# V's first weights in tiles of their own, denser fillers and a gated latent projection in a hybrid attention layer

## The chip, the cores and the metric

The kernel runs on one core of one Trainium2 chip. The metric is device time in microseconds (us): the median of several runs. The engines are TensorE (PE: matmuls; PEld: its weight loads), VectorE (DVE), ScalarE (ACT), GpSimd (POOL) and SyncE (SP), which issues the DMAs here. Each engine works through its own instruction list in order. SBUF is the on-chip memory, PSUM the accumulators that PE writes.

## The reference

One encoder layer, 1024 tokens of width 1024, all in float32. Cut to what matters:

```python
mod = silu(c) @ w_ada + b_ada;  sh_a, sc_a, g_a, sh_m, sc_m, g_m = split(mod, 6)
h = modulate(rmsnorm(x, g_attn_norm), sh_a, sc_a)
q_lat, kv_lat, k_rope, ca_qkv = split(h @ w_in)          # 256, 128, 32, 3*8*64 columns
# latent attention: 8 heads, q = norm(q_lat) @ w_q_up, k, v from norm(kv_lat) @ w_kv_up,
# rotary part of 32, QK-norm, block-causal softmax over all earlier 64-token chunks
o_mla = mla_attention(q, k, v)
# chunked attention: 8 heads of 64, QK-norm, a band of 9 chunks, relative-position bias
o_ca = chunk_attention(cq, ck, cv, rel_bias)
x = x + g_a * (concat([o_mla, o_ca]) @ w_out)
h = modulate(rmsnorm(x, g_mlp_norm), sh_m, sc_m)
u = causal_dwconv(h @ w_up, conv_w) + conv_b;  gate, val = split(u)
x = x + g_m * ((silu(gate) * val) @ w_down)
```

## The kernel before

Every float32 product is made of three matmuls. Each operand is split into a high part (rounded to the type PE takes, made by `hi_of`, L74) and the rest (`lo_of`, L82), and high x high, high x low and low x high are added up in PSUM (`gemm3`, L149). So each weight that comes from memory needs a DMA, a high part on ACT, DVE or POOL, and a low part on POOL or DVE, before PE can use it. `load_w` (L174) does that for eight slices of a weight matrix: three raw buffers (tag `wr`) take the DMAs, sixteen buffers (tag `ws`) the split slices.

The program has these stages, in order.

*Start.* The token rows are loaded and normalized, the conditioning vector's product with the first part of `w_ada` is accumulated on DVE (`ada_pair`, L249, weights by `load_ada`), and the modulated, transposed activations `hT` come out slice by slice: for each `d` from 0 to 7 PE transposes, ACT and DVE make the high parts, DVE and POOL the low parts, and PE adds slice `d` to the first query and key projection (`qk0`). Behind that loop `wv0` is loaded and split (L285): V's weights for the first two pairs of heads, with the sums of their squares (`ssw0`), from which a power-of-two scale for V is worked out (`pow2_scale`).

*Attention, with fillers.* Two lists are interleaved. One is the list of attention units. There are 16 chunked units `ca_unit(p, g, o)`: pair of heads `p` (0 to 3), half of the queries `g`, head `o` of the pair. They come in pairs (`o` = 0, 1), eight pairs in all; the seventh is `p` = 3, `g` = 0, the last `p` = 3, `g` = 1. Behind them come 16 latent units `mla_unit(gr, hh, g)`. Each unit has four tiles of 128 queries. A tile's `scores` (L717) are matmuls, a minimum on DVE, an exponential on ACT, a scaling and a split into two half-precision parts on POOL and DVE, and a transposing DMA; its `values` come some tiles later. At a unit's first tile `prep` makes its pages: queries and keys transposed by PE and split again (`ca_pages`, L690).

The other list is the fillers (L899): the V projection of the first heads (`v0`, `f_v`), query and key projections (`qk1`, `qk2`, `qk3`, `f_qk`), `v1`, the low-rank projection (`m`, `f_m`: 192 matmuls of 416 columns, then transposes of the normalized latents into `latT`), the up projections of the two groups of latent heads (`up0`, `up1`, `f_up`) and the chunked heads' part of the output projection (`oca`). Each filler is a generator that yields the cost in ns of what it has just emitted. `pace` (L936) draws from it after each tile: the tile's cost times a ratio, `R_CA` in chunked tiles and `R_MLA` in latent ones. `need` empties the list up to what a unit needs: the first latent unit needs `up0`. Two further generators ride on the fillers: `side` (`f_ada`, the rest of the conditioning, DVE steps named `aacc`) for every 1700 ns of filler, and the rotary tables (`rope_tables`, L483) with `qk1`. The latter works in 14 scratch slots on DVE, with two Sine activations on ACT.

What decides the order on an engine in the end is a scheduler at build time. It takes the order of emission as the priority; scores, softmax and values are lifted above it (`high_priority`). So a page is behind the fillers that were emitted ahead of it.

The tag `pg` has six buffers, which hold in turn rows of `x`, normalized queries and keys (`qns`), the rotary scratch and `latT` (three for each half of the tokens). The transposes of the second half in `f_m` therefore need buffers that the last chunked pages have read.

*Rest.* Output projection, gated multilayer perceptron in a seven-product (Strassen-like) form, down projection. The change doesn't touch these.

Of the kernel before, what the change touches and what calls it, by code (L numbers as in the profile page):

```python
# [12 lines left out]
F32 = mybir.dt.float32  # L13
# [10 lines left out]
P = 128  # L24
# [20 lines left out]
PSCALE, VSCALE = 2.0 ** 15, 2.0 ** 14  # L45
R_CA, R_MLA = 1.9, 0.5

# [16 lines left out]
def layer_kernel(ctx, tc, I, out):  # L64
# [108 lines left out]

    def load_w(name, src, ncol, he="a", ssw=None, jt=None):  # L174
        tiles = []
        for k in range(ND):
# [7 lines left out]
            for c0 in range(0, ncol, 256):  # L184
# [3 lines left out]
                anchor["sp"] = sp.dma_start(rw, src[:, k, c]).ins  # L188
                if jt:
                    junk = jt(f"{name}j{k}")[:, :c.stop - c0]  # L190
                    dve.tensor_tensor_reduce(junk, rw, rw, 1.0, 0.0, MUL, ADD, accum_out=ssw[:, k:k + 1])
                elif ssw is not None:
                    junk = qtile(f"{name}j{k}")
                    act.activation(junk[:, :c.stop - c0], rw, AF.Square, accum_out=ssw[:, k:k + 1])
# [9 lines left out]
    def load_ada(dd, c):  # L204
        w = st.tile([P, 2, 512], F32, name=f"adaw_{dd}_{c}", tag="wa", bufs=5)
        sp.dma_start(w[:], I["w_ada_a"][dd][:, 2 * c:2 * c + 2])
        wada[dd, c] = w
# [39 lines left out]
    ssw0 = cst.tile([P, ND], F32, name="ssw0")  # L247

    def ada_pair(dd):  # L249
        acc = rtile(f"adacc_{dd}")  # L250
# [9 lines left out]
    for d in range(ND):  # L260
        dd, half = divmod(d, 2)
        if half == 0 and dd + 1 < ND // 2:
            for c in range(4):
                load_ada(dd + 1, c)
            ada_pair(dd + 1)
        pt = ps.tile([P, 512], F32, name=f"p_ada{d}", tag="mm", bufs=2)
# [8 lines left out]
        for h in range(2):  # L275
            hT[d, h] = mod_transpose(lambda j: xs[4 * h + j][:, d * P:(d + 1) * P], d, h, 0, ps, ("T", "pv")[h], 1,
                                     hw, "hT", st, 16, "v" if h else "a", "v" if h else "p")
        for t in range(NT):
            h, j = divmod(t, 4)
# [4 lines left out]

    with tc.issue_after(anchor["lov"]), tc.issue_after(anchor["lop"]):  # L285
        wv0 = load_w("wv0_", I["w_v"][0], 256, he="v", ssw=ssw0,
                     jt=lambda n: st.tile([P, 512], F32, name=n, tag="hv", bufs=2))
    startp.__exit__(None, None, None)
# [143 lines left out]

    latT = {}

    def rope_apply(o, x, tab, t, nh, tmp, eng=pool):
# [10 lines left out]
    def f_m():  # L446
# [4 lines left out]
        for t in range(NT):  # L451
# [17 lines left out]
            lat[t] = raw  # L469
            if j == 3:  # L470
                for b in range(3):
                    ptt = ps.tile([P, 512], F32, name=f"lt_ps{h}_{b}", tag="T", bufs=TB)
# [10 lines left out]
    def rope_tables():  # L483
# [4 lines left out]
        def T():  # L488
            n = cnt[0] % 14
            cnt[0] += 1  # L490
            return buf[n // 8][:, n % 8]
# [50 lines left out]
        pi_s = 3.1415925  # L542
        sn, cn, cl, c2, cl2 = T(), T(), T(), T(), T()
        dve.tensor_scalar(cl, tot, pi_s, -pi_s, op0=MIN, op1=MAX)
        dve.tensor_scalar(c2, tot, math.pi / 2, None, op0=ADD)
        yield
        dve.tensor_scalar(cl2, (yield from reduce(c2)), pi_s, -pi_s, op0=MIN, op1=MAX)
        act.activation(sn, cl, AF.Sin)
        act.activation(cn, cl2, AF.Sin)
        yield  # L550
# [311 lines left out]
    def ca_unit(p, g, o):  # L862
        def prep():
# [8 lines left out]
            if o == 0:  # L872
                pages["c", p, g] = ca_pages(p, g)
        u = Unit(f"c{p}{o}", 64 * o, 64,
                 lambda: (pages["c", p, g][0], [pages["c", p, i][1] for i in range(g + 1)]),
# [29 lines left out]
    def fill_step():  # L905
        while fillers:
# [12 lines left out]
            if key not in ("v0", "up0", "up1", "oca"):  # L919
                nside[0] += c  # L920
                while nside[0] > 1700:
# [571 lines left out]
```

## Time and profile before

| | us |
|---|---|
| median of 3 runs | 1419.71 (1411.23 to 1421.71) |
| the profiled execution | 1410.1 |
| its span, first to last instruction | 1408.3 |
| PE busy in the span | 1234.5 |
| DVE busy | 1093.0 |
| POOL busy | 709.3 |
| ACT busy | 624.0 |

The profile is of one execution. Busy time of an engine is the union of its instructions' times. A row of the timeline gives start, duration, engine, line, operation, the tile written and those read, with the idle time before it and what ended that in brackets. A row of busy times by stretch gives, after its bounds and length, the busy time of PE, PEld, DVE, ACT and POOL with the number of instructions, then the TensorE clock that was granted (1 is full), the share of the DMA engines and GB/s. In the names `sc` are scores of chunked units, `sm` of latent ones, `ipv` and `ipq` the projections, `mp` the low-rank one, `qu` and `ku` the up projections; the numbers of buffers are left out.

The stages by the trace: the start up to 68 us, V's first projection up to 101 us, chunked units up to about 392 us, the first up projection up to 424 us, latent units up to 634 us, the output projection up to about 731 us, then the perceptron.

### The profile page before, as it was taken

What the parts mean: (1) busy time and instruction counts of PE and PEld (TensorE: products, weight loads), DVE (VectorE), ACT (ScalarE), POOL (GpSimd) and SP (SyncE); (2) the same over time, 40 slices, a digit from 0 to 9 for tenths busy, and PEclk for the clock granted to TensorE, in tenths of its full rate; (3) what the DMA queues carried; (4) which work ended last, traced back from release to release, by engine and by line L of the source; (5) the groups of instructions that cost most, each with busy time, mean ns of one, the idle gap of its engine ahead of it and who ended that gap; (6) DMA issues with size and microseconds to landing.
All of it is one profiled execution on the core that took longest, in us unless ns stands there. A gap on an engine that the chain in (4) does not pass through costs nothing.

```text
span 1408.3 us, 18699 instructions
## 1 busy us (share of the span) xinstructions
PE 1234.5 (88%) x6156; PEld 1006.3 (71%) x6156; DVE 1093.0 (78%) x1861; ACT 624.0 (44%) x1132; POOL 709.3 (50%) x685
## 2 busy tenths in 40 slices
PE   4879688989777789995677999999999999999998
PEld 3868476978655567774565887787778777888886
DVE  6847879686579997882577888988888888698667
ACT  4433545444456554652274444344434444443331
POOL 5353366375545674443563677677667874200000
PEclk9989798998888889997887999999999999999999
DMA  8223567755221478877721323333232223894451
GB/s 314 93 64 79 132 149 177 169 134 106 57 53 42 88 169 178 164 160 230 279 90 45 113 95 123 127 119 127 91 108 89 101 99 118 303 350 130 125 163 60
DMA packets 223689, 190.56 MB, mean 135 GB/s; under 512 B 148709, under 2 KB 166885, under 8 KB 223593
## 3 DMA queue, kind: packets, MB, share of 16 engines
q1 hardware_dynamic: 223592, 189.38, 47.3%
q8 instruction: 48, 0.79, 0.2%
q14 instruction: 49, 0.39, 0.1%
HBM read 117.24 MB, written 37.49 MB: 110 GB/s over the span
## 4 chain that ended last, share of the span: by engine, by line
DVE 35%; PE 30%; issue 10%; DMA 9%; POOL 8%; ACT 7%; SPq 1%; POOLq 0%; DVEq 0%; ACTq 0%
DVE u L1157 5%; DVE u L1156 4%; PE dnA_P L1304 2%; PE dnA_P L1305 2%; PE dnA_P L1306 2%; ACT u L1155 2%; DVE hlc L794 2%; PE dnB_P L1306 1%; PE dnB_P L1305 1%; PE dnB_P L1304 1%; DVE hlm L794 1%; DMA wor<-w_out 1%; DMA aw<-w_ada 1%; PE sc L740 1%; PE sm L746 1%
## 5 line engine op out<-in xcount | busy, mean ns | idle before, releaser
L76 ACT ACTIVATE dnP<-dnr 128x1024 fp32r<-128x1024 f32 x73 | 77.3, 1062 | 111.8 <-PE dnA_P L1306 43.1
L1278 DVE TENSOR_TENSOR dnP<-dnr,dnP 128x1024 fp32r<-128x1024 f32 x72 | 90.3, 1259 | 44.9 <-ACT dnP L76 43.3
L1156 DVE SCALAR_TENSOR_TENSOR u<-c,cvp,u 128x1023 f32<-128x1023 f32 x44 | 81.9, 1902 | 46.3 <-ACT u L1155 46.3
L72 POOL TENSOR_SCALAR hlm<-Pm,rim 128x512 f16<-128x512 f32 (+2 forms) x96 | 69.8, 736 | 71.8 <-DVE rim L775 28.7
L1157 DVE SCALAR_TENSOR_TENSOR u<-c,cvp,u 128x1022 f32<-128x1022 f32 x44 | 86.5, 2003 | 0.0
L72 POOL TENSOR_SCALAR hlc<-Pc,ric 128x640 f16<-128x640 f32 (+2 forms) x64 | 47.1, 738 | 71.1 <-DVE ric L775 35.4
L794 DVE SCALAR_TENSOR_TENSOR hlm<-Pm,rim,hlm 128x512 f16<-128x512 f32 (+2 forms) x96 | 65.0, 688 | 6.2 <-POOL hlm L72 5.9
L772 ACT ACTIVATE Pc<-sc,mc 128x640 f32<-128x640 f32 (+2 forms) x64 | 42.1, 658 | 54.5 <-DVE mc L761 38.9
L772 ACT ACTIVATE Pm<-sm,mm 128x128 f32<-128x128 f32 (+3 forms) x64 | 47.1, 737 | 32.0 <-DVE mm L765 18.6
L794 DVE SCALAR_TENSOR_TENSOR hlc<-Pc,ric,hlc 128x640 f16<-128x640 f32 (+2 forms) x64 | 53.0, 830 | 10.0 <-POOL hlc L72 9.3
L76 ACT ACTIVATE wc<-ws 128x512 fp32r<-128x512 f32 x22 | 13.9, 633 | 103.1 <-DVE ws L1082 103.1
L1155 ACT ACTIVATE u<-c,cvp 128x1024 f32<-128x1024 f32 x44 | 52.1, 1234 | 13.5 <-DVE c L1228 6.8
L153 PE MATMUL ipq<-wq_s,hT 128*128 128x256 f32 x192 | 56.2, 296 | 1.2 <-ACT wq_s L76 1.2
L154 PE MATMUL ipq<-wq_s,hT 128*128 128x256 f32 x192 | 56.0, 292 | 0.6 <-POOL wq_s L83 0.6
L155 PE MATMUL ipq<-wq_s,hT 128*128 128x256 f32 x192 | 56.1, 292 | 0.0
L833 PE MATMUL pvm<-PTm,vt 128*128 128x256 f16 (+1 forms) x320 | 43.2, 284 | 12.6 <-DMA PTm<-hlm 8.8
L1232 ACT ACTIVATE u<-u 128x1024 f32<-128x1024 f32 x22 | 23.3, 1061 | 67.9 <-DVE u L1157 67.9
L83 POOL TENSOR_TENSOR wc<-ws,wc 128x512 fp32r<-128x512 f32 x22 | 34.3, 1558 | 36.4 <-ACT wc L76 36.4
L1306 PE MATMUL dnA_P<-dnP 128*128 128x512 f32 x132 | 51.4, 389 | 0.0
L1305 PE MATMUL dnA_P<-dnP 128*128 128x512 f32 x132 | 51.4, 389 | 0.0
L1304 PE MATMUL dnA_P<-dnP 128*128 128x512 f32 x132 | 51.2, 389 | 0.0
L83 POOL TENSOR_TENSOR wd<-wu,wd 128x512 fp32r<-128x512 f32 x22 | 30.4, 1382 | 37.5 <-ACT wd L76 37.5
(421 smaller groups left out, 4544.6 us busy)
## 6 DMA issues: line engine op xcount, KB each, us to landing
wu<-w_up SPq DMA_DIRECT2D x44, 512.0 KB, 3.5
dnr<-g_d SPq DMA_DIRECT2D x73, 256.0 KB, 4.3
aw<-w_ada SPq DMA_DIRECT2D x48, 256.0 KB, 3.5
g_d<-u SPq DMA_DIRECT2D x22, 512.0 KB, 2.8
dnr<-w_down SPq DMA_DIRECT2D x44, 256.0 KB, 5.4
adaw<-w_ada_a SPq DMA_DIRECT2D x16, 512.0 KB, 4.9
x<-x SPq DMA_DIRECT2D x16, 512.0 KB, 8.5
g_d<-gs SPq DMA_DIRECT2D x22, 256.0 KB, 2.0
```

What stands on the lines that cost most here:

```text
L72: pool.tensor_scalar(o, i, s, 1.0, op0=MUL, op1=MUL)
L76: act.activation(o, i, AF.Copy)
L83: (pool if eng == "p" else dve).tensor_tensor(o, i, f32(hi), op=SUB)
L772: act.activation(pr[:, :n], sv, AF.Exp, bias=m[:], scale=-1.0, accum_out=rsum[:, 0:1])
L794: dve.scalar_tensor_tensor(hl[:, w:2 * w], pp, ri[:], hl[:, :w], op0=MUL, op1=SUB)
L1155: act.activation(u[:], c, AF.Identity, scale=cvp[:, cv + 2:cv + 3], bias=cvp[:, cv + 3:cv + 4])
L1156: dve.scalar_tensor_tensor(u[:, 1:], c[:, :S - 1], cvp[:, cv + 1:cv + 2], u[:, 1:], op0=MUL, op1=ADD)
L1157: dve.scalar_tensor_tensor(u[:, 2:], c[:, :S - 2], cvp[:, cv:cv + 1], u[:, 2:], op0=MUL, op1=ADD)
L1278: r = f(*a, **k)
L1304: pe.matmul(pt, sh, w[:, 0, 0], start=start, stop=False, skip_group_check=add)
L1305: pe.matmul(pt, sh, w[:, 1, 0], start=False, stop=False, skip_group_check=add)
L1306: pe.matmul(pt, sl, w[:, 0, 0], start=False, stop=stop, skip_group_check=add)
```

## The change

It has five parts. V's first weights get eight raw tiles (`wvr`, in the start's own pool), whose loads stand right behind the last conditioning weights on SP's queue; their splits (high part and sum of squares on DVE, low part on POOL) are emitted two for each `d` from 4 to 7, inside the start's loop. `R_CA` goes from 1.9 to 2.3. In `f_m`, the second half's transposes wait until the pages of the last pair of chunked units have been emitted: the generator yields -1 meanwhile, and `pace` then gives up its debt. So `up0`, which stands behind, is emitted within the last two chunked units and not ahead of the first latent unit. The rotary tables use ten scratch slots, and the arguments of the two Sines lie side by side, so that one activation does both. The argument `jt` of `load_w` goes.

```diff
-R_CA, R_MLA = 1.9, 0.5
+R_CA, R_MLA = 2.3, 0.5
...
-        sp.dma_start(w[:], I["w_ada_a"][dd][:, 2 * c:2 * c + 2])
+        anchor["ada"] = sp.dma_start(w[:], I["w_ada_a"][dd][:, 2 * c:2 * c + 2]).ins
...
+    wv0, wv0r = [], []
+
+    def wv0_load():
+        with tc.issue_after(anchor["ada"]):
+            for k in range(ND):
+                r = st.tile([P, 256], F32, name=f"wv0_r{k}", tag="wvr", bufs=8)
+                anchor["sp"] = sp.dma_start(r[:], I["w_v"][0][:, k, :]).ins
+                wv0r.append(r)
+
+    def wv0_split(k):
+        w = hw.tile([P, 2, 256], F32R, name=f"wv0_s{k}", tag="ws", bufs=16)
+        junk = st.tile([P, 512], F32, name=f"wv0_j{k}", tag="wvj", bufs=1)
+        with tc.issue_after(anchor["lov"]), tc.issue_after(anchor["lop"]):
+            hi_of("v", w[:, 0], wv0r[k][:])
+            lo_of("p", w[:, 1], wv0r[k][:], w[:, 0])
+            dve.tensor_tensor_reduce(junk[:, :256], wv0r[k][:], wv0r[k][:], 1.0, 0.0, MUL, ADD,
+                                     accum_out=ssw0[:, k:k + 1])
+        wv0.append((w[:, 0], w[:, 1]))
...
             for c in range(4):
                 load_ada(dd + 1, c)
+            if dd + 2 == ND // 2:
+                wv0_load()
             ada_pair(dd + 1)
...
+        if d >= ND // 2:
+            for k in range(2 * d - ND, 2 * d - ND + 2):
+                wv0_split(k)
...
-    with tc.issue_after(anchor["lov"]), tc.issue_after(anchor["lop"]):
-        wv0 = load_w("wv0_", I["w_v"][0], 256, he="v", ssw=ssw0,
-                     jt=lambda n: st.tile([P, 512], F32, name=n, tag="hv", bufs=2))
...
+    gate = [False]
...
             if j == 3:
+                while h and not gate[0]:
+                    yield -1
                 for b in range(3):
...
-            n = cnt[0] % 14
+            n = cnt[0] % 10
...
-        sn, cn, cl, c2, cl2 = T(), T(), T(), T(), T()
+        cl, cl2, sn, cn, c2 = buf[1][:, 2], buf[1][:, 3], buf[1][:, 4], buf[1][:, 5], T()
...
-        act.activation(sn, cl, AF.Sin)
-        act.activation(cn, cl2, AF.Sin)
+        act.activation(buf[1][:, 4:6], buf[1][:, 2:4], AF.Sin)
...
                 pages["c", p, g] = ca_pages(p, g)
+                gate[0] = (p, g) == (3, 1)
...
-                nside[0] += c
+                nside[0] += max(c, 0)
...
-            if c is None:
+            if c is None or c < 0:
```

More of the change, by code (lines that the diff above doesn't have):

```diff
@@ L171, in gemm3_f, with load_w @@
             yield 3 * len(part) * max(107, w / 2.4 + 2.5)
-    def load_w(name, src, ncol, he="a", ssw=None, jt=None):
+    def load_w(name, src, ncol, he="a", ssw=None):
         tiles = []
@@ L188, in load_w @@
                 anchor["sp"] = sp.dma_start(rw, src[:, k, c]).ins
[L189 to L192, printed above, removed]
+                if ssw is not None:
                     junk = qtile(f"{name}j{k}")
```

## Prediction

> **What bounds the kernel now.** I read the page first, then the busy time by stretch, cut where the work changes hands, then the instructions at the edges.
>
> ```profile
> span 1408.3 us, 18699 instructions
> PE 1234.5 (88%) x6156; PEld 1006.3 (71%) x6156; DVE 1093.0 (78%) x1861; ACT 624.0 (44%) x1132; POOL 709.3 (50%) x685
> ```
>
> ```profile
> core 0: us, PE busy (x) PEld busy (x) DVE busy (x) ACT busy (x) POOL busy (x), PEclk, DMA share, GB/s
> 68.00:101.00 33.00, 23.10 (x144) 20.67 (x142) 15.93 (x48) 9.78 (x21) 21.11 (x27) 0.79 0.24 73
> ...
> 283.00:320.00 37.00, 33.41 (x215) 28.62 (x213) 30.06 (x72) 15.97 (x36) 27.87 (x29) 0.94 0.56 128
> 320.00:345.00 25.00, 25.00 (x112) 20.66 (x111) 16.88 (x52) 10.14 (x44) 16.77 (x44) 0.82 0.54 120
> 345.00:365.00 20.00, 14.43 (x88) 12.21 (x87) 8.28 (x17) 8.12 (x19) 5.15 (x13) 0.95 0.29 42
> 365.00:388.00 23.00, 21.00 (x98) 16.69 (x97) 14.46 (x45) 11.98 (x37) 16.80 (x35) 0.82 0.38 80
> 388.00:432.00 44.00, 29.96 (x129) 21.57 (x128) 36.28 (x119) 23.96 (x59) 22.02 (x24) 0.84 0.25 55
> 432.00:502.00 70.00, 52.02 (x259) 40.18 (x260) 66.80 (x198) 41.34 (x96) 43.99 (x46) 0.83 0.40 85
> ```
>
> The share on the page (PE 88%) is a mean over unlike stages. From 68 to 101 us (V's first projection) no engine is busy for even three quarters of the time. From 283 to 345 us PE is nearly full. From 345 to 432 us neither PE nor DVE is (44.4 and 44.6 of 64 us up to 345-365 and 388-432, 21.0 and 14.5 of 23 between): work runs one kind after the other there. From 432 to 502 us DVE is the bound, 66.8 of 70. All edits lie before 502 us; behind that I take the kernel as it is, shifted. The edges are these rows of PE (first V product; first page of the chunked attention; its first scores; first scores of the seventh pair of chunked units; scores of the last two units when they get under way; first finished scores of the latent attention):
>
> ```profile
> 68.00 0.28 PE L153 MATMUL ipv<-wv_s,hT 128*128 128x256 f32 x1
> 68.12 0.35 PE L154 MATMUL ipv<-wv_s,hT 128*128 128x256 f32 x1
> ...
> 93.24 0.60 PE L674 MATMUL q_ps<-ident,qn 128*128 128x128 f32 x4
> ...
> 101.20 0.30 PE L740 MATMUL sc<-k,qh 128*128 128x128 f32 x1 [1.64 <-DVE k L705]
> ...
> 319.37 0.31 PE L740 MATMUL sc<-k,qh 128*128 128x128 f32 x1
> ...
> 363.71 0.47 PE L740 MATMUL sc<-k,qh 128*128 128x128 f32 x1 [1.55 <-DVE k L705]
> ...
> 424.85 0.33 PE L746 MATMUL sm<-mk,mq_0h 96*128 96x128 f32 x1 [0.46 <-DVE mk L687]
> ```
>
> **Part 1, V's first weights (-10 us).** These are the eight loads and the splits:
>
> ```profile
> L188 SPq DMA_DIRECT2D wv_r<-w_v x8: 328/328/383, 37.8 to 77.0; - x8
> L191 DVE CUSTOM_DVE_ANT_0 wv_j<-wv_r x8: 405/420/956, 66.6 to 79.8; 128x256 f32<-128x256 f32 x8
> L80 DVE CAST wv_s<-wv_r x8: 279/285/853, 66.9 to 80.1; 128x256 fp32r<-128x256 f32 x8
> L83 POOL TENSOR_TENSOR wv_s<-wv_r,wv_s x8: 724/768/1171, 67.3 to 82.1; 128x256 fp32r<-128x256 f32 x8
> ```
>
> With three raw buffers, the last load is issued at 77.0 us and the last low half starts at 82.1, so the first two V products (96 matmuls) run from 68.0 to 93.2 us. With eight buffers the loads follow the last conditioning weights on SP's queue and nothing holds them. The 96 matmuls at the pitch of the two rows above (68.00 to 68.12, 0.12 us) take 11.5 us; add 1 us for the scale's small matmul and its DVE readers, which stand between the two products. The page then starts at 80.7 instead of 93.24, a gain of 12.5. The moved loads go ahead of the first bias pair and the next projection's weights on SP's queue: eight issues of 0.328 us, 2.6 us. DVE reads the bias, in the built order, ahead of its last conditioning step; what it waits there is within the slip that follows.
>
> The splits now fall into the start, where PE sets the pace:
>
> ```profile
> 56.00:68.00 12.00, 12.00 (x103) 11.99 (x103) 7.45 (x21) 6.30 (x10) 3.43 (x5) 1.00 0.01 2
> ```
>
> DVE has 4.5 us free there and gets 8 x (0.42 + 0.285) = 5.6 us by the medians; POOL has 8.6 free and gets 8 x 0.77 = 6.2. So DVE overruns by 1 us, and by the longest rows (0.956 + 0.853 each, 14.5 us) by 10, of which some 5 could be taken before 56 us or behind the last product. Slip 0 to 6, I take 2.5: -12.5 + 2.5 = -10, ends -12.5 and -6. The longest rows fell where POOL was splitting at the same time. [...]
>
> **Part 2, one Sine instead of two (-2 us).**
>
> ```profile
> 150.81 1.28 ACT L548 ACT_TABLE_LOAD   x1
> 154.40 1.28 ACT L772 ACT_TABLE_LOAD   x1 [1.99 <-DVE mc L761]
> 166.42 1.28 ACT L549 ACT_TABLE_LOAD   x1
> 168.04 1.28 ACT L772 ACT_TABLE_LOAD   x1
> ```
>
> Each Sine costs a load to it and one back. One pair goes, 2.56 us of ACT, with the softmax of the chunked units queued behind it in ACT's order. Ends 0 and -2.9 (Sine's own 0.3 us with it); I take -2, as ACT waits near by anyway. [...] Ten scratch slots instead of 14 cost nothing: all users but the Sine are on DVE, in order.
>
> **Part 3, denser fillers (+22 us before 319, -24 us behind).** In the built program the low-rank projection has 44 of its 192 matmuls ahead of the seventh pair's first scores before the change, and 174 after; the other fillers there are the same. Earlier in the chunked units the orders hardly differ, as the weights, not the ratio, hold the fillers. The matmul's pitch:
>
> ```profile
> 377.58 0.35 PE L153 MATMUL mp<-wm_h,hT 128*128 128x416 f32 x1
> 377.77 0.35 PE L154 MATMUL mp<-wm_l,hT 128*128 128x416 f32 x1
> ```
>
> 130 x 0.19 = 24.7 us. PE idles 3.6 of 37 us in 283:320, so I take 3 as absorbed: +22. Ends +17 (twice the idle time found) and +30 (5 us of waiting for weights). Then the seventh pair and the start of the last one stand almost without fillers: before, 319.37 to 363.71 took 44.3 us. What is left is eight small tiles and the last pages. DVE has 16.88 + 8.28 us of work there, less the conditioning steps, which are now done earlier (seven in the row below, 5.2): 20, and the steps of the latent transposes in it wait at the gate now. The pace of chunked tiles with no filler stands in the second row: seven softmaxes in 24.7 us, of wider tiles, with table loads and pages among them.
>
> ```profile
> L404 DVE SCALAR_TENSOR_TENSOR aacc<-aw,cs,aacc 128x512 f32<-128x512 f32 x7 | 5.2, 746 | 0.4 <-DMA aw<-w_ada 0.4
> ...
> L772 ACT ACTIVATE Pc<-sc,mc x7: 359/793/794, 148.4 to 173.1; 128x640 f32<-128x640 f32 x5, 128x128 f32<-128x128 f32 x1, 128x256 f32<-128x256 f32 x1
> ```
>
> Between 17 and 25 I take 20, DVE's work: -24, ends -27 and -19.
>
> **Part 4, up projection beside the last two units (-13 us), its rest later (+3 us).** Before, 363.71 to 424.85 us is 61.1 us: eight tiles, then eight steps of the up projection alone. The built program now has 27 of the 72 matmuls of that projection among the last tiles and 63 of 72 ahead of the latent scores. DVE's work up to 424.85 is 14.46 + 36.28 less some 6.8 in the last 7.2 us, 44; one step of eight leaves (under 36.28 / 8 = 4.5; I take 3), so 41, and with the latent transposes' steps that now fall here 42 to 44. At the share of 432:502 (95%) 43 us takes 45; at that of 388:432 (82%) 52. I take 48: -13, ends -17 and -8. What is hidden is PE's work: 21.00 x 0.82 + 29.96 x 0.84 = 42 us at full clock, less 42 low-rank matmuls at 0.19 (8 us) that have gone, 34; it decides only if the granted clock falls under 0.7. The step that is left lands where DVE is 95% busy: +3 (0 to +5). The gate itself costs nothing on an engine: it holds back emission, and behind the closed gate stand only the latent transposes and the up projection.
>
> **Sum.** -10 - 2 + 22 - 24 - 13 + 3 = -24. The profiled run took 1410.1 us (span 1408.3 and 1.8 around it), so 1386.1; it lies 0.7% under the median of 1419.71, and scaled to that the forecast is 1395.5.
>
> **Rivals.** *The last two units and the up projection do not overlap.* Every up step waits for POOL in DVE's order, and a chunked tile behind it waits too:
>
> ```profile
> 406.47 1.65 POOL ur L117
> ```
>
> Eight such waits of 1.65 us are 13.2, the whole of part 4. Then -24 + 13 = -11, 1408.6. For it: DVE is in order, and the rows put POOL on the chain. Against: from 432 on the second up projection runs beside attention with the same waits, and DVE is 95% busy.
>
> *The early V is given back.* If the fillers of the chunked units are paced by a transfer that doesn't move with V, part 1 is lost: -14, 1405.6. For it: the second key projection is starved by its weights (first row below; 100 matmuls in 28 us). Against: those weights wait for a Square of the projection ahead, which shifts as well.
>
> *Slower: the filler block starves with attention locked behind it.* Between the first scores of the sixth pair and its key page PE now has 192 projection matmuls and 38 of the low-rank one, in its own order; tiles behind can't pass.
>
> ```profile
> 172.00:200.00 28.00, 16.64 (x100) 14.49 (x101) 0.82 (x2) 0.82 0.72 169
> 267.00:300.00 33.00, 24.55 (x189) 23.12 (x189) 1.79 (x3) 1.00 0.43 99
> ...
> L83 POOL TENSOR_TENSOR wm_l<-wm_r,wm_h x16: 520/737/1402, 266.2 to 317.8; 128x256 fp32r<-128x256 f32 x8, 128x160 fp32r<-128x160 f32 x8
> ```
>
> The block is 192 x 0.12 + 38 x 0.19 = 30 us. At the starved pace of the first row (28 us where 12 would do, 2.3 times) it takes 69: +39, so +15, 1435. It decides from 24 us of stall on. For it: the low-rank weights were split over 51 us. Against: the 189 matmuls of the second row ran at full clock, and their weights are split ahead of the block in POOL's new order too; only the last four low-rank weights wait for buffers that the block frees.
>
> That the change does nothing is excluded by the built order, where up steps do stand among the last chunked tiles.
>
> **Chances.** Forecast 0.72, no overlap 0.12, early V given back 0.10, starved block 0.06. The parts' ends added are -43 and +2; not all fall together, half way gives -34 to -11, so 1385.5 to 1408.6; the runs before spread over 10.5 us, and the two middle rivals lie within. I set 1379 to 1411. Within 1% is what a measurement of this kernel can't tell from none: 1405.5 to 1434. Faster: 0.70 of the forecast, half of the V rival, little of the first: 0.77. Same: 0.17. Slower: 0.06.
>
> **What would show it.** First chunked scores near 91 us instead of 101.2; two Sine loads less; the seventh pair's scores some 10 us later than 319 and then eight tiles in about 20 us with little on PE; latent scores near 398 instead of 425; 432:502 as full on DVE as before. The prediction is wrong if the start's last product ends beyond 72 us, if PE waits for low-rank weights inside the block, or if the last two units with seven up steps take over 56 us.

## The result, and the profile after

Taken side by side in 19 runs each, the changed kernel took 1409.99 us (median, 1405.15 to 1413.90) and the kernel before 1414.45 us (1408.14 to 1427.44): a ratio of 0.9967, 95% interval 0.9951 to 0.9982. The gain is real, but it is 4.5 us where 24 were forecast. The profiled execution took 1407.2 us, 2.9 us less than the profiled one before. The page:

```profile
span 1405.4 us, 18702 instructions
PE 1231.5 (88%) x6156; PEld 1005.2 (72%) x6156; DVE 1093.2 (78%) x1861; ACT 620.9 (44%) x1129; POOL 700.1 (50%) x685
```

Work is as before on DVE, and a little less on PE (3.0 us), ACT (3.1) and POOL (9.2); what the change did, it did by order, but for the one Sine. Busy times by stretch of the changed kernel (columns as in the prediction), cut at its own edges:

```profile
core 0: us, PE busy (x) PEld busy (x) DVE busy (x) ACT busy (x) POOL busy (x), PEclk, DMA share, GB/s
252.00:296.00 44.00, 41.77 (x320) 40.10 (x320) 22.75 (x40) 15.72 (x35) 23.30 (x30) 1.00 0.59 147
...
365.00:389.00 24.00, 20.46 (x103) 14.72 (x102) 22.15 (x77) 14.71 (x34) 9.88 (x12) 0.89 0.48 96
389.00:414.00 25.00, 18.24 (x93) 13.78 (x93) 22.68 (x71) 13.87 (x33) 12.46 (x13) 0.86 0.39 76
...
413.70:635.70 222.00, 180.08 (x966) 141.41 (x964) 184.91 (x510) 115.36 (x254) 109.30 (x132) 0.90 0.60 130
```

From 252 to 296 us PE runs hardly anything but fillers, at a granted clock of 1.00, and DVE is half idle (22.75 of 44 us busy). From 365 to 414 us, the last pair of chunked units with the up projection beside it, DVE is 91% busy (44.8 of 49), as Part 4 wanted. The last row is the latent stage, first to last latent scores; of all of it behind 502 us the prediction says only "shifted".

The edges, in rows of PE of the changed kernel (first V product; first query page; first key page; first chunked scores; the last scores of the fifth pair's first unit; the last transpose of the sixth pair's key page; the scores that waited for it; the last two latent transposes of the first half; the seventh pair's query page and first scores; the last pair under way; first finished latent scores):

```profile
71.67 0.28 PE L153 MATMUL ipv<-wv_s,hT 128*128 128x256 f32 x1
...
83.83 0.60 PE L694 MATMUL q_ps<-ident,qn 128*128 128x128 f32 x4
...
94.49 0.60 PE L694 MATMUL k_ps<-ident,qn 128*128 128x128 f32 x4
...
96.73 0.30 PE L760 MATMUL sc<-k,qh 128*128 128x128 f32 x1 [0.93 <-DVE k L725]
...
232.06 0.49 PE L760 MATMUL sc<-k,ql 64*128 64x512 f32 x1
...
289.66 0.27 PE L694 MATMUL k_ps<-ident,qn 128*128 128x128 f32 x1
...
294.63 0.22 PE L760 MATMUL sc<-k,qh 128*128 128x128 f32 x1
...
331.71 0.60 PE L495 MATMUL lt_ps<-ident,lat 128*128 128x128 f32 x4
...
334.01 0.61 PE L495 MATMUL lt_ps<-ident,lat 128*128 128x128 f32 x4
...
340.86 0.60 PE L694 MATMUL q_ps<-ident,qn 128*128 128x128 f32 x4
...
346.85 0.45 PE L760 MATMUL sc<-k,qh 128*128 128x128 f32 x1 [1.64 <-DVE k L725]
...
363.88 0.90 PE L760 MATMUL sc<-k,qh 128*128 128x512 f32 x2 [0.18 <-ACT Pc L792]
...
413.38 0.22 PE L766 MATMUL sm<-mk,mq_0h 96*128 96x128 f32 x1
```

Three rows of PE before (the same scores of the fifth pair, the sixth pair's key page, the scores behind that page):

```profile
248.03 0.49 PE L740 MATMUL sc<-k,ql 64*128 64x512 f32 x1
...
277.82 0.60 PE L674 MATMUL k_ps<-ident,qn 128*128 128x128 f32 x4
...
282.33 0.33 PE L740 MATMUL sc<-k,qh 128*128 128x128 f32 x1 [0.17 <-DVE k L705]
```

Read against the rows of the prediction, the lead (minus is earlier) runs like this. First V product +3.7, first page -9.4, first scores -4.5, fifth pair -16.0, scores behind the sixth pair's key page +12.3, seventh pair +27.5, last pair under way +0.2, first latent scores -11.5. The end of the last latent scores came at 635.7 us against 633.4, so +2.3, and the stretch behind it, the output projection above all, gave 5 us back, for a reason that stays open: the span is 2.9 us shorter. So the larger part of the error, 15.5 us, lies ahead of the latent scores (-11.5 where -27 stood in the sum), and 10.9 us in the latent stage, which took 222.0 us instead of 208.1 (+13.9 where +3 stood).

### The profile page after: what moved, and what is told of

Same layout as the page of the kernel before. It is cut to its first block, busy times and chain, and to the rows that moved or that the text cites. A ratio compares the mean times of both kernels' runs of the same rounds, so it can differ in the third digit from the quotient of the medians.

```text
span 1405.4 us, 18702 instructions
## 1 busy us (share of the span) xinstructions
PE 1231.5 (88%) x6156; PEld 1005.2 (72%) x6156; DVE 1093.2 (78%) x1861; ACT 620.9 (44%) x1129; POOL 700.1 (50%) x685
## 4 chain that ended last, share of the span: by engine, by line
DVE 21%; PE 20%; issue 6%; POOL 5%; ACT 4%; DMA 2%; SPq 0%; DVEq 0%; POOLq 0%; ACTq 0%
DVE u L1178 5%; DVE u L1177 4%; PE dnA_P L1325 2%; PE dnA_P L1326 2%; PE dnA_P L1327 2%; ACT u L1176 2%; PE dnB_P L1326 1%; PE dnB_P L1325 1%; PE dnB_P L1327 1%; DVE u L1254 1%; DVE c L1249 1%; DVE gmbc L1164 1%; DVE wu L1105 1%; PE p L1088 1%; PE p L1086 1%
## 5 line engine op out<-in xcount | busy, mean ns | idle before, releaser
L1299 DVE TENSOR_TENSOR dnP<-dnr,dnP 128x1024 fp32r<-128x1024 f32 x72 | 90.4, 1260 | 44.9 <-ACT dnP L76 44.2
L72 POOL TENSOR_SCALAR hlm<-Pm,rim 128x512 f16<-128x512 f32 (+2 forms) x96 | 66.0, 695 | 86.8 <-DVE rim L795 18.2
L72 POOL TENSOR_SCALAR hlc<-Pc,ric 128x640 f16<-128x640 f32 (+2 forms) x64 | 48.4, 760 | 84.2 <-DVE ric L795 32.3
L814 DVE SCALAR_TENSOR_TENSOR hlm<-Pm,rim,hlm 128x512 f16<-128x512 f32 (+2 forms) x96 | 68.3, 719 | 12.6 <-POOL hlm L72 12.2
L853 PE MATMUL pvm<-PTm,vt 128*128 128x256 f16 (+1 forms) x320 | 46.7, 293 | 24.9 <-DMA PTm<-hlm 24.8
L853 PEld LDWEIGHTS <-vt 128*128 128x128 f16 x320 | 31.6, 108 | 40.5 <-DMA PTm<-hlm 22.6
L76 ACT ACTIVATE wc<-ws 128x512 fp32r<-128x512 f32 x22 | 13.9, 633 | 102.0 <-DVE ws L1103 98.7
```

Of the source, the lines that this page charges most:

```text
L72: pool.tensor_scalar(o, i, s, 1.0, op0=MUL, op1=MUL)
L76: act.activation(o, i, AF.Copy)
L814: dve.scalar_tensor_tensor(hl[:, w:2 * w], pp, ri[:], hl[:, :w], op0=MUL, op1=SUB)
L853: last = pe.matmul(dst, u.vst(j), mov, start=(x == 0), stop=(x == len(todo) - 1), skip_group_check=True)
L1299: r = f(*a, **k)
```

## The experiments

Fifteen kernels. For each the trace gives the ends of the same tiles; us from the start of the span, "stage" being last minus first latent scores. (The expectations call the first tile of the sixth pair its fifth, as tiles are counted through both halves of the queries.) One trace stands for each kernel, while the runs of one kernel, where there are several, spread over 3 to 10 us (those of the kernel before up to 19), so a difference of a few us between two traces shows nothing by itself; the traced run of kernel 4 is the slowest of its five, 7.8 us above their median.

| | time, ratio to before | first scores | 5th pair, first unit | 7th pair, first tile | last pair, first tile | first latent | last latent | stage |
|---|---|---|---|---|---|---|---|---|
| before | 1 | 101.8 | 248.5 | 320.1 | 365.0 | 425.3 | 633.4 | 208.1 |
| changed | 0.9967 | 97.3 | 232.6 | 347.7 | 365.6 | 413.7 | 635.7 | 222.0 |
| 1 V alone | 1.0051 | 96.0 | 242.7 | 314.0 | 358.8 | 420.5 | 641.2 | 220.7 |
| 2 denser and gate, no V | 1.0132 | 102.0 | 254.4 | 357.0 | 376.3 | 428.4 | 651.2 | 222.8 |
| 3 second up projection late | 1.0076 | 96.2 | 231.6 | 346.1 | 364.1 | 412.3 | 642.2 | 229.9 |
| 4 latent transposes in `mm` | 0.9893 | 96.7 | 233.9 | 324.5 | 355.8 | 411.4 | 624.6 | 213.2 |
| 5 all pages lifted | 0.9892 | 96.0 | 228.3 | 338.9 | 356.4 | 404.5 | 622.8 | 218.3 |
| 6 both halves gated | 0.9909 | 95.7 | 232.9 | 323.2 | 361.2 | 413.7 | 623.5 | 209.8 |
| 7 as 4, latent pages lifted | 0.9897 | 95.7 | 235.7 | 323.4 | 354.4 | 407.3 | 623.3 | 216.0 |
| 8 as 4, chunked pages lifted | 0.9897 | 96.5 | 226.2 | 295.9 | 320.3 | 396.1 | 619.3 | 223.2 |
| 9 changed, latent values later | 0.9963 | 96.4 | 233.8 | 349.3 | 367.3 | 415.4 | 634.7 | 219.3 |
| 10 as 8, values four tiles behind | 0.9849 | 96.4 | 223.6 | 292.7 | 317.1 | 392.9 | 614.8 | 221.9 |
| 11 as 8, five tiles | 0.9822 | 95.5 | 227.5 | 296.5 | 319.4 | 399.2 | 614.3 | 215.1 |
| 12 as 11, V's scale step lifted | 0.9775 | 90.7 | 219.7 | 286.2 | 312.8 | 389.3 | 601.1 | 211.8 |

**1. V's first weights alone.** The kernel before with the loads and splits of the change, and nothing else of it.

> V's first weights alone (eight raw buffers, loads behind the conditioning weights, splits in the start's last four steps); ratio of fillers, gate and Sines as before. Theory A (what is early at the first chunked scores is kept): first chunked scores near 97 instead of 101 us, and some 5 us kept to the end, 1409.5 (0.9965). Rival (the fillers of the chunked units are paced by weights that do not move, so early V is given back): first chunked scores near 97 too, but the seventh pair's scores at 319 +- 2 and the time 1414 (1.000 +- 0.0015).

Measured: ratio 1.0051 (1.0028 to 1.0075), slower. Up to the first latent scores theory A holds: 5.8 us early at the first scores, 6.1 at the seventh pair's, 4.8 at the latent ones. In the total neither theory does. Then the latent stage takes 12.6 us more than before, though its units and fillers are emitted in the same sequence; only the order that the build made of them differs.

**2. Denser fillers and gate without V.**

```diff
-R_CA, R_MLA = 1.9, 0.5
+R_CA, R_MLA = 2.3, 0.5
```

and the gate's lines, on the kernel before.

> Denser fillers and the gate without V's part, with two Sines as before. Theory A (V's part is worth 5 us, the denser fillers next to nothing): 1414 to 1416 (1.000). Rival (V is given back, the whole gain of the change is the fillers'): 1410 (0.997). In both the seventh pair's scores come 25 us or more later than before's 319, if it is the denser order that delays them.

Measured: 1.0132 (1.0111 to 1.0154), so slower than either theory. The seventh pair comes 36.9 us late. Some of that is new: the fourth pair's key page stands behind all of a projection (its last transposes, and the scores that wait for them).

```profile
208.58 0.60 PE L677 MATMUL k_ps<-ident,qn 128*128 128x128 f32 x4
...
212.02 0.33 PE L743 MATMUL sc<-k,qh 128*128 128x128 f32 x1 [1.72 <-DVE k L708]
```

In the changed kernel that page was through at 177.0 us. V and the denser fillers do not add: 1.0051 and 1.0132 alone, 0.9967 together (with the one Sine). A split of the gain into parts can't be read off such runs; only off the edges inside them.

**3. The second up projection held back.** In the changed kernel half of it is emitted among the last chunked tiles. A second gate keeps it behind the first latent unit:

```diff
+        while gr and not gate2[0]:
+            yield -1
...
             if i % 4 == 0:
+                gate2[0] = not u.band
                 need(u.need)
```

> The changed kernel, with the second up projection held back until the first latent unit, so that it and the out-projection fillers are emitted among the latent tiles where they were before the change. Theory B (the 17 us lost between 563 and 636 us come from where the out-projection products of the fillers stand in PE's order): the latent scores start as in the changed kernel (414), the lead over before stays near 12 us to the last latent scores (near 622), and the time is 1402 to 1404 (0.992). Rival (latent stage bound by an engine or the transfers, a lead there is always given back): the last latent scores at 633 to 636 again and 1410 (0.997).

Measured: 1.0076 (1.0048 to 1.0103), the stage 229.9 us. The theory falls, and the rival's numbers (633 to 636 us, 0.997) aren't met either: with the fillers emitted where they were before, the stage is longest of all. DVE has 193.1 us of work in it instead of 184.9 and is idle for 36.8, as long as in the changed kernel (37.1).

**4. Latent transposes out of the pages' buffer.** The pages of attention and the transposes `lt_ps` share one PSUM buffer, tag `T`. Denser fillers emit `lt_ps` of the first half ahead of the seventh pair's pages, and so its page waits until four low-rank steps are normalized and transposed: in the rows above, 334.01 ahead of 340.86.

```diff
-                    ptt = ps.tile([P, 512], F32, name=f"lt_ps{h}_{b}", tag="T", bufs=TB)
+                    ptt = ps.tile([P, 512], F32, name=f"lt_ps{h}_{b}", tag="mm", bufs=2)
```

> The changed kernel, with the PSUM tiles of the latent transposes taken from the two buffers of the projections instead of the one buffer that the attention pages use. Theory C (the seventh pair's query page waits for that one buffer, which the three latent transposes take first, and these wait for four low-rank steps): the seventh pair's scores within 8 us of the sixth pair's last ones (27 us in the changed kernel), so near 325 instead of 347; the low-rank steps four to seven move behind them, the latent scores some 4 us earlier, 1405 (0.9935). Rival (the projection work in front is what takes the time, whatever the buffer): seventh pair's scores 340 or later, time as the changed kernel, 1410.

Measured: 0.9893 (0.9870 to 0.9916). The key page and the first scores of the seventh pair in its trace:

```profile
317.58 0.60 PE L694 MATMUL k_ps<-ident,qn 128*128 128x128 f32 x4
...
323.92 0.33 PE L760 MATMUL sc<-k,qh 128*128 128x128 f32 x1 [1.59 <-ACT Pc L792]
```

They come 3.9 us behind the sixth pair's last, and 23 us earlier than in the changed kernel: theory C. But the latent scores start only 2.3 us earlier, since the low-rank steps that stood in front now stand behind. The other 8.8 us of the 11.1 gained by the last latent scores are a shorter latent stage (213.2), which theory C doesn't explain.

**5. All pages lifted** to the priority of the scores, in the changed kernel.

```diff
-                u.prep()
+                with tc.high_priority(offset=OFF_S):
+                    u.prep()
```

> The changed kernel, with the attention pages (the transposes of queries and keys and what follows them) at the priority of the scores, so that they no longer stand behind products of the fillers that were emitted before them. Theory D (the changed kernel's losses are key pages standing behind filler blocks in PE's order: 43 us inside the sixth pair's fifth tile, 6 us at the latent tile of 574 us): the sixth pair's fifth tile done by 262 us instead of 295, the sixth pair over by 285 instead of 320; the fillers pile up ahead of the seventh pair, which stays near 345; the latent stage takes at most 210 us instead of 222; time 1398 (0.989). Rival (the order only shifts the work about): latent stage 218 to 225 us, time 1410 or more.

Measured: 0.9892 (0.9861 to 0.9924). Ahead of the latent stage it went as theory D said: the sixth pair's first tile done at 251.2 us, the pair over at 276.7, the seventh at 338.9, first latent scores 9.2 us earlier than in the changed kernel. Its stage, 218.3, is the rival's.

**6. Both halves gated**, with the single buffer.

```diff
-                while h and not gate[0]:
+                while not gate[h]:
                     yield -1
...
-                gate[0] = (p, g) == (3, 1)
+                gate[0], gate[1] = p == 3, (p, g) == (3, 1)
```

> The changed kernel, with the first half's latent transposes gated too, until the seventh pair's pages are emitted; the page buffer stays the single one. Theory C (the order in that one buffer delayed the seventh pair, not its number): seventh pair's first scores within 8 us of the sixth pair's last, near 325, as with the transposes in the projections' buffers; time 1396 to 1401 (0.990). Rival (the gain came from two buffers for the latent transposes): seventh pair's scores near 325 too, but the transposes with one buffer stall the tail, 1407 or more (0.997).

Measured: 0.9909 (0.9878 to 0.9941), the seventh pair 3.8 us behind the sixth. So it was the sequence in that buffer. The latent scores start at 413.7 us, just as in the changed kernel: holding the seventh pair for 23 us had cost nothing that shows there. The whole gain is the stage (209.8), which the edit doesn't explain.

**7 and 8. Pages lifted in part**, on the kernel of 4: those of the latent units, and those of the chunked ones.

> The kernel with the latent transposes in the projections' buffers, and the pages of the latent units at the priority of the scores. Theory D: first to last latent scores at most 206 us (213 there, 222 in the changed kernel, 208 before), time 1389 (0.985). Rival (the latent stage's length is set by where the out-projection products stand, and the pages are not what waits): 212 us or longer, 1396 or more.

Measured: 0.9897 (0.9869 to 0.9925), stage 216.0. Theory D falls for the latent stage: its pages are not what makes it long.

> The kernel with the latent transposes in the projections' buffers, and the pages of the chunked units alone at the priority of the scores. Theory D: first scores near 92 us instead of 97, as the first key page no longer stands behind 36 products of V; sixth pair's fifth tile done by 262 us; first latent scores at 405 or earlier (411 there), time 1390 (0.986). Rival (PE's and DVE's work up to the latent stage is conserved, attention that runs ahead leaves the up projection alone at the end): first latent scores 411 or later, 1397 or more.

Measured: 0.9897 (0.9853 to 0.9940). The sixth pair's key page and the scores behind it:

```profile
243.83 0.27 PE L694 MATMUL k_ps<-ident,qn 128*128 128x128 f32 x1
...
248.35 0.23 PE L760 MATMUL sc<-k,qh 128*128 128x128 f32 x1
```

46 us earlier than in the changed kernel (289.66 and 294.63), and 15.3 us of it against kernel 4 are still there at the first latent scores. So a key page behind a filler block does cost time. The first scores did not move (96.5): they wait for something else, see 12. And the stage takes 223.2, so 5.3 us are left of the 15.3 in these two traces, and by the ratios (0.9893 and 0.9897) nothing.

**9 to 11. Latent value products later.** PE waits 14.5 us in the changed kernel's latent stage for transposed probabilities, 3.4 before. I counted, in the built order, how many later score tiles stand ahead of each pair's value products, and that count went with the stage's length over the first ten kernels (4.28 for 208.1 us, 4.25 for 209.8, 4.19 for 213.2, 4.06 for 216.0, and 3.56 to 3.78 for 218 to 230). So the products were emitted later and kept behind the newest scores:

```diff
-        if n >= DEPTH:
-            u, i = tiles[n - DEPTH]
+        while nv < len(tiles) and nv + (DEPTH if tiles[nv][0].band else 5) <= n:
+            u, i = tiles[nv]
+            nv += 1
...
+                if not u.band:
+                    pin.enter_context(tc.issue_after(lastsc[-1]))
```

> The changed kernel, with the value products of the latent units emitted five tiles behind their scores instead of three and kept behind the newest score tile in PE's order. Between a pair of latent score tiles and its value products PE's order holds on average 4.28 later score tiles before the change, 3.56 in the changed kernel, 4.19 in the one with the latent transposes in the projections' buffers, 3.69 in the one with chunked pages lifted; here 4.84. Theory F (the latent stage's length follows this number, since value products that wait for their transposed probabilities at the head of PE's queue hold the scores behind them): first to last latent scores at most 209 us instead of 222, PE's waits of value products for transposes under 9 us instead of 14.5, time 1396 (0.989). Rival (the stage is set by DVE's and ACT's softmax work or by the out-projection's place): 216 us or longer, 1404 or more.

> The kernel with lifted chunked pages and the latent transposes in the projections' buffers, with the latent value products four tiles behind and kept behind the newest score tile: 4.19 later score tiles in PE's order instead of 3.69. Theory F: latent stage 211 to 214 us instead of 223, time 1385 (0.981). Rival: 219 us or longer, 1392 or more.

> The same with five tiles: 5.00 later score tiles. Theory F: latent stage at most 208 us, time 1380 (0.978), if not the last value products, now two tiles later, add a few us at the end. Rival: 219 us or longer, 1392 or more.

Measured: stages of 219.3, 221.9 and 215.1; ratios 0.9963 (0.9946 to 0.9981), 0.9849 (0.9813 to 0.9886) and 0.9822 (0.9783 to 0.9860). The waits for transposes did fall, to 9.3, 7.4 and 4.3 us, and others took their place. In 9 and 10 the stage is the rival's, in 11 it lies between the two. Theory F falls as a rule: counts of 4.84, 4.19 and 5.00 all gave a longer stage than kernel 4 has at 4.19, so a count that fitted ten kernels did not hold once it was set on purpose.

**12. V's scale step lifted**, on 11.

```diff
-                vscale["c", pp] = pow2_scale(f"c{pp}", ssw[:], hb[:], ND, 2.0 * D)
+                with tc.high_priority(offset=0 if pp else OFF_S):
+                    vscale["c", pp] = pow2_scale(f"c{pp}", ssw[:], hb[:], ND, 2.0 * D)
```

> The same with five tiles, and V's scale step (a sum on PE, a power on POOL, small steps on DVE) at the priority of the scores. In the changed kernel that power stood on POOL behind two other powers and three low halves, 4.5 us after its input, and V's evacuation and the first key page behind it. Theory H (this is where half of V's 9.4 us went between the first page and the first scores): first chunked scores near 92.5 us instead of 96.5, some 4 us of it kept at the first latent scores, time 4 us under the kernel with five tiles. Rival (the first key page waits for something else, the single page buffer or ACT): first scores within 1 us of 96.5.

Measured: 0.9775 (0.9743 to 0.9807), the fastest. First POOL in the changed kernel, then POOL and PE in this one (vsc is V's scale, `q_ps`, `k_ps` the first pages):

```profile
76.76 3.25 POOL L117 TENSOR_TENSOR r<-ss,nhalf 128x8 f32<-128x8 f32 x2
79.97 0.73 POOL L83 TENSOR_TENSOR wq_s<-wq_r,wq_s 128x256 fp32r<-128x256 f32 x1
80.79 0.52 POOL L116 TENSOR_SCALAR ss<-ss 128x8 f32<-128x8 f32 x1
81.39 0.74 POOL L83 TENSOR_TENSOR wq_s<-wq_r,wq_s 128x256 fp32r<-128x256 f32 x1
82.09 0.56 POOL L321 TENSOR_TENSOR vsc<-vsc,nhalf 128x1 f32<-128x1 f32 x1
```

```profile
74.44 0.55 POOL L322 TENSOR_TENSOR vsc<-vsc,nhalf 128x1 f32<-128x1 f32 x1
...
82.47 0.60 PE L696 MATMUL q_ps<-ident,qn 128*128 128x128 f32 x4
...
87.93 0.60 PE L696 MATMUL k_ps<-ident,qn 128*128 128x128 f32 x4
...
90.17 0.30 PE L762 MATMUL sc<-k,qh 128*128 128x128 f32 x1 [1.64 <-DVE k L727]
```

The power that ran at 82.09 us runs at 74.44, the key page follows the query page by 5.5 us instead of 10.7 (9.3 in 11), and the first scores come 4.8 us earlier than in 11. Theory H holds. At the latent scores it is 9.9 us; how much of the rest is order by chance isn't known.

**13 to 15. The latent stage without the out-projection.** The fillers `oca` (192 products) are held until the last latent tile is emitted, in the kernel before, the changed one and kernel 8.

```diff
     def f_oca():
+        while hold[0]:
+            yield -1
...
+    hold[0] = False
     need(["oca"])
```

> The kernel before, with the out-projection fillers (192 products of 0.235 us, 45 us) held back until the last latent tile is emitted. Theory I (the place of these products in PE's order makes the latent stage 208, 222 or 223 us long): without them the three kernels' stages lie within 4 us of each other, near 195 us (DVE's 184 and little idle time). Rival (the order of attention's own pieces and of the second up projection makes it): the spread stays 10 us or more, this one the shortest. The products then run alone behind the stage, so the time itself goes up by some 30 us, 1445.

> The changed kernel, with the same fillers held back. Theory I: the stage within 4 us of that of the kernel before without them, near 195 us; rival: 10 us or more longer. Time near 1430 by theory I, 1440 by the rival.

> The kernel with lifted chunked pages and the latent transposes in the projections' buffers, with the same fillers held back. Theory I: the stage within 4 us of that of the kernel before without them, near 195 us; rival: 10 us or more longer. Time near 1412 by theory I, 1425 by the rival.

One run each. Busy times of the latent stage, first with the fillers in it (before; kernel 2; kernel 8), then without (before; changed; kernel 8):

```profile
425.30:633.40 208.10, 175.99 (x952) 137.66 (x952) 184.23 (x505) 112.78 (x248) 115.96 (x132) 0.91 0.64 134
```

```profile
428.40:651.20 222.80, 181.10 (x952) 141.31 (x952) 184.76 (x501) 113.20 (x249) 111.90 (x131) 0.89 0.59 126
```

```profile
396.10:619.30 223.20, 180.26 (x952) 140.22 (x952) 186.02 (x505) 112.79 (x249) 110.28 (x131) 0.89 0.60 126
```

```profile
429.40:635.10 205.70, 156.93 (x782) 119.04 (x782) 185.09 (x510) 102.50 (x229) 105.58 (x128) 0.80 0.58 111
```

```profile
413.30:622.90 209.60, 151.70 (x788) 116.06 (x787) 183.88 (x514) 103.99 (x233) 105.28 (x128) 0.82 0.56 109
```

```profile
399.90:610.70 210.80, 157.30 (x785) 119.35 (x785) 183.59 (x508) 102.73 (x229) 106.29 (x128) 0.80 0.55 108
```

Two things are to be seen. Kernels 2 and 8 were built, as it happens, with the same order of matmuls on PE from the end of the fifth latent unit on, and nearly so ahead of it. They start the stage 32.3 us apart and take 222.8 and 223.2 us for it. For these two, what the stage costs is in its built order, not in when it is reached. And without the out-projection the three stages lie within 5.1 us (205.7, 209.6, 210.8) where they lay within 15.1 (208.1, 222.0, 223.2): with these fillers in it the kernel before takes 2.4 us more and the other two 12.4 each. The spread is theory I's (5 us where 4 were expected, 10 by the rival); the level is 206 to 211, not 195. But holding the fillers back (21 to 24 of the 192 products still ran in the stage) re-dealt the order of attention's own products too: the count of runs 9 to 11 is 4.31, 4.09 and 4.22 here, where it was 4.28, 3.56 and 3.69. So it is likely, and not shown, that the fillers' place makes the 10 us. The times were 1448.46, 1434.92 and 1422.91 us: with the fillers out of the way the changed kernel is 13.5 us ahead of the one before, and it was 16.1 us ahead at the first latent scores and 12.2 at the last.

## Why the prediction was wrong

The sum up to the latent scores was -27 and came out at -11.5: -4.5 for -10 at the first scores; +32.0 for +20 (part 3's +22 and the Sine's -2) from there to the seventh pair; -27.3 for -24 to the last pair; -11.6 for -13 to the latent scores. The latent stage then took +13.9 for +3. Three steps failed: the first of part 3, what is behind 502 us, and the one from the first page to the first scores in part 1.

**Part 1, V (-10; at the first scores -4.5).** The page came 9.4 us early, as worked out. The start slipped by 3.7 us where 2.5 were taken, because the splits ran long beside each other (operation, count, shortest, median and longest in ns, first and last start):

```profile
L80 DVE CAST wv_s<-wv_r x8: 281/820/1379, 55.3 to 70.1; 128x256 fp32r<-128x256 f32 x8
...
L83 POOL TENSOR_TENSOR wv_s<-wv_r,wv_s x8: 738/858/867, 56.8 to 71.0; 128x256 fp32r<-128x256 f32 x8
...
L261 DVE CUSTOM_DVE_ANT_0 wv_j<-wv_r x8: 409/414/987, 56.7 to 70.9; 128x256 f32<-128x256 f32 x8
```

The median CAST went from 285 to 820 ns: the five long ones all started while POOL was subtracting, the three of under 0.3 us while it was idle. The two long sums of squares (0.99 and 0.96 us) also started while POOL was subtracting, the other six (0.41 to 0.42 us) while it was idle. Why DVE's instructions run long beside a subtraction on POOL no run here shows. PE waited 2.9 us for POOL's low halves of `hT` from 40 us to the first V product, where it had waited 1.0 before. What failed is the next step, that first scores follow the page as before. The prediction gave "1 us for the scale's small matmul and its DVE readers" and left out the power on POOL between those readers. It stood behind two other powers and two low halves there, since the scale is now asked for while the query norms still run. Run 12 shows it: 4.8 us against kernel 11.

**Part 2, one Sine (-2).** One pair of table loads has gone, 1.28 us each; these two are left in the rotary tables (ACT, changed kernel):

```profile
155.24 1.28 ACT L569 ACT_TABLE_LOAD   x1
...
161.33 1.28 ACT L792 ACT_TABLE_LOAD   x1
```

ACT is busy 3.1 us less in all. No run took this edit by itself, so its share of the time stays open.

**Part 3, denser fillers (+22, -24).** The first half is the step that failed most: it took the extra products times their pitch, less 3 us that PE's idle time would absorb. From the first scores to the seventh pair (before; changed; kernel 8):

```profile
101.80:320.10 218.30, 191.42 (x1291) 163.10 (x1291) 168.56 (x470) 101.15 (x234) 115.72 (x137) 0.90 0.59 136
```

```profile
97.30:347.70 250.40, 221.51 (x1455) 190.79 (x1455) 176.62 (x487) 112.61 (x287) 137.18 (x200) 0.93 0.56 128
```

```profile
96.50:295.90 199.40, 188.51 (x1261) 160.09 (x1261) 168.74 (x472) 98.99 (x229) 108.05 (x133) 0.92 0.66 151
```

PE's busy time grew by 30.1 us where 24.7 were reckoned, and its idle time rose from 26.9 to 28.9 us instead of falling by 3. I counted products ahead of the seventh pair and not what they hold: the sixth pair's key page and its scores stand behind 230 of them (12.3 us late), and the seventh pair's query page behind three transposes in one buffer (23 us, runs 4 and 6). With the chunked pages lifted, PE idles 10.9 us in this stretch. Up to the latent scores it idles 44.9 us before, 41.8 in the changed kernel, 37.3 in kernel 4 and 26.4 in kernel 8: the idle time that the change was to fill was mostly left, and lifting the pages over the fillers is what lowered it.

"Earlier in the chunked units the orders hardly differ" failed too: from the first scores to the fifth pair the lead grew from 4.5 to 16.0 us, where V alone kept its 5.8 and the denser order alone came 5.9 us late (run 2). But this gain was mostly work put off: 77 products of V had run there by the end of the fifth pair's first unit, where 152 had before, and 75 of them at 0.12 us (68.00 to 68.12 in the prediction's rows) are 9 us. They are among the 43.5 us that the stretch from the fifth to the seventh pair then lost.

The second half, the rest of the seventh pair without fillers, gave 27.3 where 24 were taken: right. The hold of 23 us itself cost the latent scores 0 to 2.3 us, for PE was busy with work that was due anyway.

**Part 4, up projection beside the last pair (-13, +3).** Right: from 363.88 to 413.38 us are 49.5 us where 48 were forecast and 61.1 stood before, so -11.6, and DVE is 91% busy between the two shares that were weighed. The rival of no overlap is out. What was left over took 5.9 us by the 20th latent tile (lead 11.6 to 5.7), more than the 3 taken, though by the 24th tile the lead was back at 12.3.

**Behind 502 us "the kernel as it is, shifted".** This is the step that took all of what was left. The lead, grown to 15.3 us at the tenth latent unit, was 12.2 us at the end of the eleventh and 0.1 us one tile on. That tile's rows:

```profile
573.26 0.50 PE L153 MATMUL oc<-wo,ch 128*128 128x512 f32 x1 [3.34 <-ACT ch L76]
...
580.87 0.60 PE L694 MATMUL mk_ps<-ident,kn 128*96 128x128 f32 x4
...
582.23 0.75 DVE L707 SCALAR_TENSOR_TENSOR mk<-mk_ps,gk_m,mk 96x512 fp32r<-96x512 f32 x1 [6.27 <-ACT mk L706]
```

PE waits 3.3 us for an out-projection operand that has just been loaded, 18 of the out-projection's products run with eight of scores and values between them, and behind them stands the key page that the next scores need; DVE, the busiest engine of the stage (184.9 of 222.0 us), is idle for 6.3 us. That is one place of several: DVE's work is 184 us in both stages, its idle time 24 before and 37 after. The kernel before had the shortest stage of all that were run with these fillers in it; the other 13 took 1.7 us (run 6) to 21.8 us (run 3) more. V alone, which emits the same units and fillers there, lost 12.6 us, and two builds with one order of PE took the same time for the stage (222.8 and 223.2). So no cost of the change's own shows there; it lost an order that happened to be good. That the out-projection's place carries some 10 of the 14 us is likely (runs 13 to 15) and not shown, since attention's own order moved with it. What distinguishes a good order from a bad one stays open: the second up projection's time of emission, lifted pages and later value products were tried and none of them explains it. A kernel with the stage's order of before forced on it was not tried.

None of the rivals is what happened. The one nearest in its number, no overlap (1408.6), is out by part 4. Early V was not given back (1405.6): V alone kept 4.8 us to the latent scores. The block of 230 products did lock attention behind it, as the slower rival said, but it wasn't starved: from 252.4 to 289.7 us PE was busy for 35.1 of 37.3 us at a granted clock of 1.00.

## What to carry over

In a kernel whose engines run an order made at build time, an edit upstream re-deals the order downstream. Read the built order of each later stage before calling it "shifted", and judge a part by edges inside the trace, not by the total: here two parts that each cost time alone gained together. When fillers get denser, list what each block of them stands in front of, single buffers included: the fastest kernel (0.9775) is the changed one with its chunked pages and V's scale step lifted over the fillers, the latent transposes out of the pages' buffer, and the latent value products moved back. How much of its gain is a good order by chance isn't known.

## What was not expected of the hardware

In the changed kernel a power of 128x8 elements took POOL 1.65 us (two in 3.25), more than twice the 0.73 us of the low half of a 128x256 weight slice behind them, so two row norms held its queue for over 3 us.

A CAST on DVE that started while POOL was subtracting ended only behind the subtraction, after 0.82 us where the one before it took 0.28. In the changed kernel (POOL, then the two CASTs on DVE):

```profile
69.96 0.87 POOL L83 TENSOR_TENSOR wv_s<-wv_r,wv_s 128x256 fp32r<-128x256 f32 x1 [0.83 <-DVE wv_s L80]
```

```profile
69.60 0.28 DVE L80 CAST wv_s<-wv_r 128x256 fp32r<-128x256 f32 x1
...
70.14 0.82 DVE L80 CAST wv_s<-wv_r 128x256 fp32r<-128x256 f32 x1
```

The second CAST starts while POOL subtracts and ends 0.1 to 0.2 us behind the subtraction; so do the other four long ones of V's weights. Beside a power the CASTs did not run long: in the trace before, four CASTs that started while POOL was at a power took 0.28 to 0.29 us.

In runs 13 to 15, without most of the out-projection's products, the granted clock of the latent stage was lower: 0.80 instead of 0.91 in the kernel before (782 matmul records instead of 952), 0.82 instead of 0.90 in the changed one (788 instead of 966) and 0.80 instead of 0.89 in kernel 8 (785 instead of 952). DVE's work there was 185.1, 183.9 and 183.6 us, where it had been 184.2, 184.9 and 186.0.
